# Hybrid decoder layer on one core: the output projection's weights placed and split beside the last branch map

## The chip, the core and the metric

The kernel runs on one core of a Trainium2 chip. The metric is the time of one execution on the device in microseconds (us), as the median of several runs; less is better. TensorE is called PE, VectorE DVE, ScalarE ACT, GpSimd POOL, and SyncE, which issues the loads, SP. The span is the stretch from the first to the last instruction of the profiled execution.

## What is computed

One layer on 256 tokens of width 4096, in float32. The parts that matter here:

```python
proj = rmsnorm(x, norm_g) @ w_in                    # 4096 -> 12288 columns, cut into eight sections
ya = conv_branch(a_val, a_glu, ...) @ a_pw          # width 1536: the big branch map, 1536 x 1536
ya = ya * silu(a_gate)
yb = gmlp_branch(b_u, b_v, ...) * silu(b_gate)      # width 1280
yc = pool_branch(c_in, c_w, ...) * silu(c_gate)     # width 1280
x = x + concat([ya, yb, yc]) @ w_out                # 4096 x 4096: the output projection
return rmsnorm(x, final_g)
```

## The kernel before

**Products in three passes.** Each float32 operand is split into two rounded parts: `hi`, a cast on ACT (L217 for weights, L291 for activations), and `lo`, the rest, a subtraction on DVE (L218, L292). A product is three matmuls of 128 x 128 by 128 x 512: hi·hi, hi·lo and lo·hi (L337 to L339; L864 to L866 in the paired columns). PE so reads weights only after ACT and then DVE have gone over them.

**Streaming.** Weights come in loads of 128 x 2048 floats, 1 MB (`Source.load`, L206). `stream` cuts a load into two sub-blocks of 1024 columns, splits each (`split`) and puts its use into a list `pending`, whose first entry is used when it holds more than AHEAD = 2. A sub-block is two input tiles of 128, for two groups of 128 tokens: 12 matmuls. In the front of the kernel the weights' pool `wpool` holds 4 raw loads and 3 split sub-blocks; in the back `wpool2` holds 3 raw loads and HELD = 5 split sub-blocks. The program is written in this order, and a scheduler then orders each engine's instructions by priority and by what they depend on. On the chip each engine goes through its own queue in order.

**Stages.** The input projection, the branches' element-wise work, the pooling branch's map, and then the big branch map `w_pw`: three groups of 512 columns, each six sub-blocks, from `project_rows` in a loop over `c0`. A group's result is multiplied into `a_gate` (L778), turned by transposes on PE (`turned`, L314) and split (L291, L292): these are `ya`, the last of the 32 input tiles of the output projection. Behind the loop stand `drain()`, which uses what is pending, `finish_all()`, and the closing of all pools of the front; only then are the back's pools opened: `xn` (the residual rows), `wpool2`, and the PSUM banks `q1` to `q8`.

**Output projection.** `first_columns` does columns 0 to 511: 16 sub-blocks, 192 matmuls, accumulated in banks `q2` and `q4`. In its course it makes eight `combine`s, sums of neighbouring activation blocks (L852, L856, L858, L859), and loads the residual rows (`load_rows`, L820 and L821). `rows_done` adds the result into `xn` on DVE (L829), squares it on ACT (L830), which frees the bank, and scales it (L835). `paired_columns` then does 1024 columns at a time, three times; in half of its steps seven products take the place of eight (a Strassen scheme), for which DVE also adds weight blocks (`w_sums`, L936 to L939). The last 512 columns are done in three pieces, with the final norm behind each token group: mean, square root on ACT (L975), reciprocal and scaling on DVE (L974 to L986), and the stores.

The square root's function table is loaded at the first use; `nc.scalar.activation(out=ssq[:, 0, 8:9], ..., func=AF.Sqrt)` (L813) is there for that alone.

Of the kernel before, what the change touches and what calls it, by code (L numbers as in the profile page):

```python
# [34 lines left out]
TAPS = 31  # L35
PAD = TAPS - 1
# [42 lines left out]
C_GROUP = W_C // len(POOL_WINDOWS)  # L79


OUT_BLOCKS = [0, 1, 2, 3, 4, 5, 6, 7]


PAIRED = [1, 3, 5, 6, 8, 10, 11, 13]


# [10 lines left out]
def trunk(ctx: ExitStack, tc: tile.TileContext, x, xt, params, w1, wv, w2, w_pw, w_c, w_o, wst, bbias, blg, blb, fg, out):  # L98
    nc = tc.nc

    const = ctx.enter_context(tc.tile_pool(name="const", bufs=1))
    acts = ctx.enter_context(tc.tile_pool(name="acts", bufs=1))
    front_ctx = ExitStack()
    weights = {"pool": front_ctx.enter_context(tc.tile_pool(name="wpool", bufs=1)), "raw": 4, "parts": 3}
    ps_acc = front_ctx.enter_context(tc.tile_pool(name="ps_acc", bufs=6, space=PSUM))
    ps_aux = front_ctx.enter_context(tc.tile_pool(name="ps_aux", bufs=2, space=PSUM))

    def raw_tile(name):
        return weights["pool"].tile([P, 2048], F32, tag="raw", name=name, bufs=weights["raw"])
# [49 lines left out]
    def finish_all():  # L159
        while urgent or slow:  # L160
            clock[0] += 1
            run_one()
# [25 lines left out]
    def drain():  # L188
        while pending:
            use_next()  # L190

    class Source:
# [6 lines left out]
        def load(self, n, parts=None):  # L199
            t = raw_tile("w_raw")  # L200
            at = 0
            if self.order:
                self.at = self.order.popleft() * P * 2048
            for w in parts or [n]:
                src = self.ap[self.at : self.at + P * w].rearrange("(p n) -> p n", p=P)
                nc.sync.dma_start(out=t[:, at : at + w], in_=src)  # L206
                last_load[:] = traced()[-1:]
                self.at += P * w
                at += w
            return t  # L210
# [152 lines left out]
    u_b = mid.tile([P, 2, W_B], F32, name="u_b")  # L363
    v = mid.tile([P, 2, W_B], F32, tag="m2", name="v")
    ws_sb = mid.tile([P, W_B], F32, tag="m3", name="ws_sb")
    h_a = mid.tile([P, TA, PAD + S], F32, tag="m1", name="h_a")
    late, tasks = {}, {}

    nc.gpsimd.memset(h_a[:, :, :PAD], 0.0)
# [102 lines left out]

    def post_a_gate(pss, col, o, w):
        if "a_gate" not in late:
            late["a_gate"] = mid.tile([P, 2, W_A], F32, tag="m1", name="a_gate")
        for c in range(2):
            yield from silu(late["a_gate"][:, c, col : col + w], pss[c][:, o : o + w], c)

# [303 lines left out]
        return evacuate  # L782

    src_pw = Source(w_pw)
    for c0 in range(0, W_A, 512):
        project_rows(src_pw, h_hl, 512, evacuate_pw(c0))
    drain()
    finish_all()
    mid_ctx.close()
    tmp_ctx.close()  # L790
    front_ctx.close()


    def back(**kw):
        return ctx.enter_context(tc.tile_pool(bufs=1, reuse_waits="tile", **kw))

    outp = back(name="outp")
    xn = outp.tile([P, 2, D], F32, name="xn")
    weights.update(pool=back(name="wpool2"), raw=3, parts=HELD)
    sums = weights["pool"]  # L800
    combos = [sums.tile([P, 4, 2, P], F32R, name=f"combo{i}") for i in range(len(PAIRED))]
    fin = back(name="fin")
    ssq = fin.tile([P, 2, 9], F32, name="ssq")
    ps_out = back(name="ps_out", space=PSUM)

    def bank(i):
        return ps_out.tile([P, 512], F32, tag=f"q{i}", name=f"q{i}", bufs=1)

    y_all = yb + yc + ya
    y_hl = [y_all[4 * b + i] for b in OUT_BLOCKS for i in range(4)]  # L810
    src_o = Source(w_o, [8 * g + b for g in (0, 7) for b in OUT_BLOCKS])

    nc.scalar.activation(out=ssq[:, 0, 8:9], in_=ones[:, :1], func=AF.Sqrt)  # L813
    LAST = D - 512
    fg_bc = {}

# [16 lines left out]
    def rows_done(c, ps, c0):  # L833
        z = add_rows(c, ps, c0, 512, c0 // 512)
        nc.vector.tensor_tensor(out=z, in0=z, in1=fg_bc[c0], op=ALU.mult)  # L835

    def scratch(name):

        return sums.tile([P, 4, 512], F32, tag="sums", name=name, bufs=1)

# [27 lines left out]
    def paired_columns(g):  # L868
# [51 lines left out]
        for p in range(KT // 2):  # L920
            if p == 4:
                load_rows(g * 512)
                load_rows((g + 1) * 512)
            raw = raw_tile("w_raw")
            for h in range(2):
                at = ((g + h) * 8 + OUT_BLOCKS[p // 2]) * P * 2048
                src = w_o[at : at + P * 2048].rearrange("(p n) -> p n", p=P)
                nc.sync.dma_start(out=raw[:, h * 1024 : (h + 1) * 1024], in_=src[:, (p % 2) * 1024 : (p % 2 + 1) * 1024])
            if p not in PAIRED:
                for h in range(2):  # L930
                    feed(*split(raw[:, h * 1024 : (h + 1) * 1024]), lambda a, b, p=p, h=h: plain(p, h, (a, b)))
                continue
            w = raw.rearrange("p (b n) -> p b n", b=4)
            s = scratch("w_sums")
            w57 = s[:, :2]
            nc.vector.tensor_tensor(out=w57, in0=w[:, 0::3], in1=w[:, 2:3].broadcast_to([P, 2, 512]), op=ALU.add)  # L936
            feed(*split(raw[:, :1024]), lambda a, b, p=p: seven(p, (1, 2), (a, b)))
            nc.vector.tensor_tensor(out=s[:, 2], in0=s[:, 0], in1=w[:, 3], op=ALU.add)
            nc.vector.tensor_tensor(out=s[:, 3], in0=s[:, 2], in1=w[:, 1], op=ALU.add)  # L939
            feed(*split(raw[:, 1536:]), lambda a, b, p=p: seven(p, (3,), (a, b)))  # L940
            flat = s.rearrange("p b n -> p (b n)")
            feed(*split(flat[:, :1024]), lambda a, b, p=p: seven(p, (5, 7), (a, b)))
            feed(*split(flat[:, 1024:]), lambda a, b, p=p: seven(p, (6, 4), (a, b)))

    def first_columns():

        acc = [bank(i) for i in (2, 4)]
        todo = deque(range(len(PAIRED)))

        def use(k0, nk, hi, lo):  # L950
            for c in range(2):
                for i in range(nk):
                    k = k0 + i
                    rows_product(acc[c], c, hi, lo, y_hl[k], i, 0, 512, k == 0, k == KT - 1)
            if todo and k0 % 4 == 2:
                combine(todo.popleft())
            if k0 == 8:
                load_rows(0)

        stream(src_o, KT, 512, use)  # L960
        drain()
        for c in range(2):
            rows_done(c, acc[c], 0)

    def mean_so_far(c, n):
        a = fin.tile([P, 1], F32, tag="fin_a", name="fin_a", bufs=2)
# [145 lines left out]
```

## Time and profile before

| | |
|---|---|
| median of 3 runs | 1380.23 us (1379.55 to 1381.44) |
| the profiled execution's own time | 1379.32 us |
| its span | 1377.6 us |
| mean granted clock of PE | 0.993 |
| busy, share of the span | PE 99%, PE weight loads 82%, DVE 75%, ACT 49% |
| moved by DMA | 281.01 MB, mean 204 GB/s |

A share of busy time is a mean over stages, so the views by stage and the timelines say more. In a timeline a row begins with its start (us from the start of the span) and its duration; `x2` says that two instructions were merged, and the bracket at the end how long the engine was idle before and what ended that. Matmuls overlap: one of 512 columns has a duration of 0.39 us, but at full clock the next one starts 0.23 us later, so times of PE are taken from start to start. `w_hi<-w_raw` is a cast of weights, `ps_acc` and `q` are accumulators.

### The profile page before, as it was taken

What the parts mean: (1) busy time and instruction counts of PE and PEld (TensorE: products, weight loads), DVE (VectorE), ACT (ScalarE), POOL (GpSimd) and SP (SyncE); (2) the same over time, 40 slices, a digit from 0 to 9 for tenths busy, and PEclk for the clock granted to TensorE, in tenths of its full rate; (3) what the DMA queues carried; (4) which work ended last, traced back from release to release, by engine and by line L of the source; (5) the groups of instructions that cost most, each with busy time, mean ns of one, the idle gap of its engine ahead of it and who ended that gap; (6) DMA issues with size and microseconds to landing.
All of it is one profiled execution on the core that took longest, in us unless ns stands there. A gap on an engine that the chain in (4) does not pass through costs nothing.

```text
span 1377.6 us, 16339 instructions
## 1 busy us (share of the span) xinstructions
PE 1357.2 (99%) x6224; PEld 1129.5 (82%) x6224; DVE 1034.3 (75%) x1468; ACT 677.5 (49%) x806; POOL 5.7 (0%) x52
## 2 busy tenths in 40 slices
PE   9999999999999999999999999999979999999996
PEld 7888888888988888888888888888868888888886
DVE  7568888888888887786447744567568899999974
ACT  8654444444445443564344443455444565656642
POOL 0000000000000000000000000000000000000000
PEclk9999999999999999999999999999989999999998
DMA  9975555555556555554555555555518755666663
GB/s 348 344 264 184 187 192 201 183 188 202 192 200 192 202 194 186 195 199 155 186 194 198 184 193 204 184 187 172 213 66 300 254 202 205 216 211 221 216 221 123
DMA packets 56591, 281.01 MB, mean 204 GB/s; under 512 B 8640, under 2 KB 12096, under 8 KB 31168
## 3 DMA queue, kind: packets, MB, share of 16 engines
q1 hardware_dynamic: 56368, 279.95, 57.8%
q8 instruction: 48, 0.79, 0.2%
q14 instruction: 31, 0.25, 0.1%
q10 hardware_dynamic: 144, 0.02, 0.0%
HBM read 275.75 MB, written 4.19 MB: 203 GB/s over the span
## 4 chain that ended last, share of the span: by engine, by line
PE 96%; DVE 2%; DMA 1%; ACT 0%; issue 0%; SPq 0%; DVEq 0%; ACTq 0%
PE ps_acc L338 24%; PE ps_acc L339 24%; PE ps_acc L337 24%; PE q L864 6%; PE q L865 6%; PE q L866 6%; PE q L338 2%; PE q L339 2%; PE q L337 2%; DMA gb<-in_blb_dram 1%; PE ps_aux L314 1%; DVE w_lo L218 0%; DVE xn L983 0%; DMA w_raw<-in_w_dram 0%; PE ps_aux L390 0%; PE ps_aux L612 0%
## 5 line engine op out<-in xcount | busy, mean ns | idle before, releaser
L218 DVE TENSOR_TENSOR w_lo<-w_raw,w_hi 128x1024 fp32r<-128x1024 f32 (+1 forms) x495 | 589.3, 1196 | 290.5 <-ACT w_hi L217 289.1
L217 ACT CAST w_hi<-w_raw 128x1024 fp32r<-128x1024 f32 (+1 forms) x495 | 506.3, 1030 | 563.2 <-PE ps_acc L339 315.1
L337 PE MATMUL ps_acc<-w_hi,act 128*128 128x512 f32 (+2 forms) x1504 | 578.4, 385 | 0.7 <-ACT w_hi L217 0.7
L338 PE MATMUL ps_acc<-w_lo,act 128*128 128x512 f32 (+2 forms) x1504 | 577.6, 384 | 0.4 <-DVE w_lo L218 0.3
L339 PE MATMUL ps_acc<-w_hi,act 128*128 128x512 f32 (+2 forms) x1504 | 577.8, 384 | 0.0
L338 PEld LDWEIGHTS ps_acc<-w_lo,act 128*128 128x128 f32 x1504 | 282.7, 188 | 56.4 <-DVE w_lo L218 1.7
L337 PEld LDWEIGHTS ps_acc<-w_hi,act 128*128 128x128 f32 x1504 | 282.5, 188 | 55.8 <-ACT w_hi L217 0.9
L339 PEld LDWEIGHTS ps_acc<-w_hi,act 128*128 128x128 f32 x1504 | 282.6, 188 | 55.1
L524 DVE SCALAR_TENSOR_TENSOR c_a<-h_a,par,c_a 128x256 f32<-128x256 f32 x360 | 153.7, 479 | 0.0
L864 PE MATMUL q<-w_hi,act 128*128 128x512 f32 x264 | 102.8, 390 | 0.0
L865 PE MATMUL q<-w_lo,act 128*128 128x512 f32 x264 | 102.7, 389 | 0.0
L866 PE MATMUL q<-w_hi,act 128*128 128x512 f32 x264 | 102.6, 389 | 0.0
L217 ACT CAST w_hi<-w_sums 128x1024 fp32r<-128x1024 f32 x48 | 50.6, 1054 | 55.7 <-DVE w_sums L939 28.1
L218 DVE TENSOR_TENSOR w_lo<-w_sums,w_hi 128x1024 fp32r<-128x1024 f32 x48 | 58.3, 1222 | 5.7 <-ACT w_hi L217 4.8
L337 PE MATMUL q<-w_hi,act 128*128 128x256 f32 (+1 forms) x160 | 56.3, 353 | 4.3 <-ACT w_hi L217 4.3
L864 PEld LDWEIGHTS q<-w_hi,act 128*128 128x128 f32 x264 | 49.5, 188 | 10.8 <-ACT q L830 0.6
L866 PEld LDWEIGHTS q<-w_hi,act 128*128 128x128 f32 x264 | 49.6, 188 | 10.4
L338 PE MATMUL q<-w_lo,act 128*128 128x256 f32 (+1 forms) x160 | 56.5, 353 | 1.5 <-DVE w_lo L218 1.5
L865 PEld LDWEIGHTS q<-w_lo,act 128*128 128x128 f32 x264 | 49.5, 188 | 10.1
L339 PE MATMUL q<-w_hi,act 128*128 128x256 f32 (+1 forms) x160 | 56.2, 351 | 0.0
L337 PEld LDWEIGHTS q<-w_hi,act 128*128 128x128 f32 x160 | 30.7, 193 | 8.5 <-ACT w_hi L217 4.5
L865 PE MATMUL q<-w_lo,combo 128*128 128x512 f32 x96 | 37.3, 389 | 0.0
(145 smaller groups left out, 664.5 us busy)
## 6 DMA issues: line engine op xcount, KB each, us to landing
w_raw<-in_w_dram SPq DMA_DIRECT2D x149, 1024.0 KB, 4.8
w_raw<-in_w_o_dram SPq DMA_DIRECT2D x96, 512.0 KB, 4.7
w_raw<-in_wv_dram SPq DMA_DIRECT2D x20, 1024.0 KB, 4.8
w_raw<-in_w_o_dram SPq DMA_DIRECT2D x16, 1024.0 KB, 5.6
w_raw<-in_w_pw_dram SPq DMA_DIRECT2D x9, 1024.0 KB, 4.8
x_rows<-in_x_dram SPq DMA_DIRECT2D x4, 1024.0 KB, 6.8
xn<-in_x_dram SPq DMA_DIRECT2D x8, 512.0 KB, 8.3
out_dram<-xn SPq DMA_DIRECT2D x6, 512.0 KB, 3.3
```

What stands on the lines that cost most here:

```text
L217: nc.scalar.copy(out=hi[:, w], in_=raw[:, w])
L218: nc.vector.tensor_tensor(out=lo[:, w], in0=raw[:, w], in1=f32(hi[:, w]), op=ALU.subtract)
L314: nc.tensor.transpose(ps[:, c * P : (c + 1) * P], rows[:, c, m * P : (m + 1) * P], ident)
L337: nc.tensor.matmul(ps[:, :w], lhsT=act[:, c, 0], rhs=hi, start=f, stop=False)
L338: nc.tensor.matmul(ps[:, :w], lhsT=act[:, c, 0], rhs=lo, start=False, stop=False)
L339: nc.tensor.matmul(ps[:, :w], lhsT=act[:, c, 1], rhs=hi, start=False, stop=l)
L524: nc.vector.scalar_tensor_tensor(out=c_a[:, m], in0=src, scalar=w, in1=c_a[:, m], op0=ALU.mult, op1=ALU.add)
L864: nc.tensor.matmul(ps, lhsT=ahi, rhs=hi, start=f, stop=False)
L865: nc.tensor.matmul(ps, lhsT=ahi, rhs=lo, start=False, stop=False)
L866: nc.tensor.matmul(ps, lhsT=alo, rhs=hi, start=False, stop=l)
```

## The change

All pools of SBUF's front that live until the last branch map (`wpool`, and a new pool `gate` for `h_a` and `a_gate`) are laid out from the right end. The middle pools lie at the left and are closed when the projection of group 1 has been written, before group 2's; `wpool2` is opened there at once, and the output projection's loads and splits follow the branch map in the stream, without `drain()` and `finish_all()`. `first_columns` accumulates in the front's PSUM pool. At its fourth sub-block (`k0 == 6`) it calls `branches_done`, which closes the front's pools and opens those of `xn`, the combinations and the final norm; the square root's first use stands there too. Combinations are made at `k0` = 10, 12, ..., 24 instead of 2, 6, ..., 30, and `load_rows(0)` at 12 instead of 8. Each load gets an ordering dependency, without a semaphore, on the one before. `OUT_BLOCKS`, the numbers 0 to 7 in order, is dropped. The diff without that and without renamings:

```diff
-    weights = {"pool": front_ctx.enter_context(tc.tile_pool(name="wpool", bufs=1)), "raw": 4, "parts": 3}
-    ps_acc = front_ctx.enter_context(tc.tile_pool(name="ps_acc", bufs=6, space=PSUM))
-    ps_aux = front_ctx.enter_context(tc.tile_pool(name="ps_aux", bufs=2, space=PSUM))
+    front_ctx, ps_ctx = ExitStack(), ExitStack()
+    weights = {"pool": front_ctx.enter_context(tc.tile_pool(name="wpool", bufs=1, side="right")), "raw": 4, "parts": 3}
+    gate = front_ctx.enter_context(tc.tile_pool(name="gate", bufs=1, side="right"))
+    ps_acc = ps_ctx.enter_context(tc.tile_pool(name="ps_acc", bufs=6, space=PSUM))
+    ps_aux = ps_ctx.enter_context(tc.tile_pool(name="ps_aux", bufs=2, space=PSUM))
...
+                if last_load:
+                    tc.add_manual_dep(traced()[-1], last_load[0].name, ISSUE_ORDER, reason="in the order of use")
                 last_load[:] = traced()[-1:]
...
     for c0 in range(0, W_A, 512):
         project_rows(src_pw, h_hl, 512, evacuate_pw(c0))
-    drain()
-    finish_all()
-    mid_ctx.close()
-    tmp_ctx.close()
-    front_ctx.close()
+        if c0 == 512:
+            finish_urgent()
+            mid_ctx.close()
+            tmp_ctx.close()
...
     weights.update(pool=back(name="wpool2"), raw=3, parts=HELD)
...
+    def branches_done():
+
+        nonlocal outp, fin, xn, ssq
+        finish_urgent()
+        assert not slow and len(ya) == TA
+        y_hl.extend(ya)
+        front_ctx.close()
+        outp = back(name="outp")
+        xn = outp.tile([P, 2, D], F32, name="xn")
+        combos.extend(outp.tile([P, 4, 2, P], F32R, name=f"combo{i}") for i in range(len(PAIRED)))
+        fin = back(name="fin")
+        ssq = fin.tile([P, 2, 9], F32, name="ssq")
+        nc.scalar.activation(out=ssq[:, 0, 8:9], in_=ones[:, :1], func=AF.Sqrt)
...
     def first_columns():

-        acc = [bank(i) for i in (2, 4)]
+        nonlocal ps_out
+        acc = [ps_acc.tile([P, 512], F32, name="ps_acc") for _ in range(2)]
         todo = deque(range(len(PAIRED)))

         def use(k0, nk, hi, lo):
+            if k0 == 6:
+                branches_done()
...
-            if todo and k0 % 4 == 2:
+            if todo and k0 >= 10:
                 combine(todo.popleft())
-            if k0 == 8:
+            if k0 == 12:
                 load_rows(0)
...
         for c in range(2):
             rows_done(c, acc[c], 0)
+        ps_ctx.close()
+        ps_out = back(name="ps_out", space=PSUM)
```

The lines of the changed kernel lie a little further down: L217 and L218 are L218 and L219 there, L291 is L292, L314 is L315, L337 to L339 are L338 to L340, L778 is L779, L813 is L819, L829 and L835 are L840 and L846, L936 to L939 are L947 to L950.

**ACT, from the branch map's last group to the output projection.** `w_hi` are casts of weights; those from `w_raw_7940` and `w_raw_7950` are the first of the output projection. Before:

```order
L217 CAST w_hi_7844<-w_raw_7826 128x1024
L291 CAST act_7781<-ps_aux_7778 128x2x128
L291 CAST act_7787<-ps_aux_7784 128x2x128
L291 CAST act_7889<-ps_aux_7886 128x2x128
L291 CAST act_7895<-ps_aux_7892 128x2x128
L291 CAST act_7901<-ps_aux_7898 128x2x128
L291 CAST act_7907<-ps_aux_7904 128x2x128
L858 CAST combo0_7922<-a_full_7984 128x4x128
L217 CAST w_hi_7942<-w_raw_7940 128x1024
L217 CAST w_hi_7946<-w_raw_7940 128x1024
L858 CAST combo1_7923<-a_full_8027 128x4x128
L217 CAST w_hi_7952<-w_raw_7950 128x1024
```

Now, in the middle of the last group (`w_raw_7870`, `w_raw_7930` and `w_raw_7964` are output weights, `w_raw_7735` and `w_raw_7795` branch map weights):

```order
L218 CAST w_hi_7737<-w_raw_7735 128x1024
L218 CAST w_hi_7872<-w_raw_7870 128x1024
L218 CAST w_hi_7753<-w_raw_7735 128x1024
L218 CAST w_hi_7888<-w_raw_7870 128x1024
L218 CAST w_hi_7932<-w_raw_7930 128x1024
L218 CAST w_hi_7797<-w_raw_7795 128x1024
L218 CAST w_hi_7948<-w_raw_7930 128x1024
```

The first output casts stood behind the last conversions and the first combination's cast; now they alternate with the casts of the branch map's last group; four of them stand in these rows and a fifth (`w_hi_7966`) a little further down the queue, all ahead of the last four conversions. DVE's subtractions moved in the same way. The load of the square root's table and its first use (L819) moved from the start of the program to the place just ahead of those four conversions.

**PE, from the last matmul of the branch map on.** `ps_aux` are transposes of the gated result, accumulators `q2` and `q4` (before) and `ps_acc_7868` and `ps_acc_7869` (now) belong to the output projection. Before:

```order
L339 MATMUL ps_acc_7803<-w_hi_7844,act_7081 128x512
L314 MATMUL ps_aux_7886<-ident_74,a_gate_6657 128x128
L314 MATMUL ps_aux_7892<-ident_74,a_gate_6657 128x128
L314 MATMUL ps_aux_7886<-ident_74,a_gate_6657 128x128
L314 MATMUL ps_aux_7892<-ident_74,a_gate_6657 128x128
L314 MATMUL ps_aux_7898<-ident_74,a_gate_6657 128x128 x2
L314 MATMUL ps_aux_7904<-ident_74,a_gate_6657 128x128 x2
L337 MATMUL q2_7938<-w_hi_7942,act_7219 128x512
L337 MATMUL q4_7939<-w_hi_7942,act_7219 128x512
```

Now:

```order
L340 MATMUL ps_acc_7808<-w_hi_7849,act_7084 128x512
L315 MATMUL ps_aux_7906<-ident_77,a_gate_6660 128x128
L315 MATMUL ps_aux_7912<-ident_77,a_gate_6660 128x128
L338 MATMUL ps_acc_7868<-w_hi_7872,act_7222 128x512
L339 MATMUL ps_acc_7868<-w_lo_7873,act_7222 128x512
L340 MATMUL ps_acc_7868<-w_hi_7872,act_7222 128x512
L315 MATMUL ps_aux_7906<-ident_77,a_gate_6660 128x128
L315 MATMUL ps_aux_7912<-ident_77,a_gate_6660 128x128
L338 MATMUL ps_acc_7868<-w_hi_7872,act_7228 128x512
L339 MATMUL ps_acc_7868<-w_lo_7873,act_7228 128x512
L340 MATMUL ps_acc_7868<-w_hi_7872,act_7228 128x512
L338 MATMUL ps_acc_7869<-w_hi_7872,act_7222 128x512
```

The eight transposes stood in one block ahead of the first output matmul; now output matmuls stand between them.

**DVE, at the end of `first_columns`.** `a_full` and `combo` are combinations, `w_sums` the paired columns' weight sums. Before:

```order
L856 TENSOR_TENSOR a_full<-a_full 128x128 x2
L218 TENSOR_TENSOR w_lo<-w_raw,w_hi 128x1024
L859 TENSOR_TENSOR combo_7929<-a_full,combo_7929 128x4x128
L936 TENSOR_TENSOR w_sums<-w_raw 128x1024
L218 TENSOR_TENSOR w_lo<-w_raw,w_hi 128x1024
L938 TENSOR_TENSOR w_sums<-w_sums,w_raw 128x512
L939 TENSOR_TENSOR w_sums<-w_sums,w_raw 128x512
L218 TENSOR_TENSOR w_lo<-w_raw,w_hi 128x1024
L218 TENSOR_TENSOR w_lo<-w_raw,w_hi 128x512
L829 TENSOR_TENSOR xn<-q_7938,xn 128x512
L829 TENSOR_TENSOR xn<-q_7939,xn 128x512
L835 TENSOR_TENSOR xn<-xn,fg_bc 128x512
```

Now:

```order
L867 TENSOR_TENSOR a_full<-a_full 128x128 x2
L219 TENSOR_TENSOR w_lo<-w_raw,w_hi 128x512
L867 TENSOR_TENSOR a_full<-a_full 128x128
L840 TENSOR_TENSOR xn<-ps_acc,xn 128x512
L867 TENSOR_TENSOR a_full<-a_full 128x128
L840 TENSOR_TENSOR xn<-ps_acc,xn 128x512
L846 TENSOR_TENSOR xn<-xn,fg_bc 128x512
L870 TENSOR_TENSOR combo_7999<-a_full,combo_7999 128x4x128
L846 TENSOR_TENSOR xn<-xn,fg_bc 128x512
L947 TENSOR_TENSOR w_sums<-w_raw 128x1024
```

The weight sums of the first pair stood ahead of the two additions into `xn`; now they stand behind them and behind the eighth combination.

## Rows read from the trace of the kernel before

**Rows 1.** chain of waits that ended last, share of the span by engine (the page)

```profile
PE 96%; DVE 2%; DMA 1%; ACT 0%; issue 0%; SPq 0%; DVEq 0%; ACTq 0%
```

**Rows 2.** busy time by stage: us; PE, PEld, DVE, ACT, POOL (instructions); PEclk; DMA; GB/s

```profile
1000.00:1021.60 21.60, 21.60 (x103) 17.23 (x102) 12.15 (x17) 7.93 (x13) 0.00 (x0) 1.00 0.19 80
1021.60:1031.50 9.90, 2.69 (x11) 1.13 (x9) 7.48 (x20) 5.01 (x9) 0.00 (x0) 0.65 0.00 0
...
1036.00:1076.40 40.40, 40.40 (x180) 33.27 (x178) 34.66 (x61) 18.91 (x23) 0.00 (x0) 1.00 0.87 312
1076.40:1166.00 89.60, 89.60 (x395) 73.94 (x395) 83.41 (x93) 52.73 (x63) 0.00 (x0) 1.00 0.61 208
1166.00:1248.00 82.00, 82.00 (x364) 67.89 (x363) 80.03 (x89) 49.20 (x58) 0.00 (x0) 1.00 0.63 213
```

**Rows 3.** the same view in steps of 2 us at the seam

```profile
1024.00:1026.00 2.00, 0.45 (x4) 0.20 (x2) 1.45 (x5) 0.71 (x2) 0.00 (x0) 0.63 0.00 0
1026.00:1028.00 2.00, 0.00 (x0) 0.00 (x0) 1.19 (x5) 0.88 (x2) 0.00 (x0) 0.50 0.00 0
...
1034.00:1036.00 2.00, 2.00 (x9) 1.59 (x8) 2.00 (x3) 0.40 (x1) 0.00 (x0) 0.81 0.76 307
```

**Rows 4.** PE timeline: start us, us, engine line op out<-in [idle before <-releaser]

```profile
1021.25 0.40 PE L339 MATMUL ps_acc<-w_hi,act 128*128 128x512 f32 x1
1021.48 0.38 PE L314 MATMUL ps_aux<-ident,a_gate 128*128 128x128 f32 x2
1022.42 0.44 PE L314 MATMUL ps_aux<-ident,a_gate 128*128 128x128 f32 x2 [0.56 <-DVE a_gate L778]
1023.67 0.77 PE L314 MATMUL ps_aux<-ident,a_gate 128*128 128x128 f32 x4 [0.81 <-DVE act L292]
1028.74 1.22 PE L337 MATMUL q<-w_hi,act 128*128 128x512 f32 x2 [4.29 <-ACT w_hi L217]
1031.50 0.80 PE L338 MATMUL q<-w_lo,act 128*128 128x512 f32 x1 [1.54 <-DVE w_lo L218]
...
1034.66 0.45 PE L337 MATMUL q<-w_hi,act 128*128 128x512 f32 x1
...
1076.22 0.84 PE L864 MATMUL q<-w_hi,act 128*128 128x512 f32 x2
...
1081.98 0.39 PE L864 MATMUL q<-w_hi,act 128*128 128x512 f32 x1
```

**Rows 5.** load queue's timeline, and time to landing of line L206's loads, 985 to 1036

```profile
992.99 39.95 SPq L206 DMA_DIRECT2D w_raw<-in_w_o_dram  x4
...
DMA to landing us min/median/max: 4.7/6.9/12.2
```

**Rows 6.** timelines of ACT and DVE at the seam

```profile
1022.79 0.65 ACT L291 CAST act<-ps_aux 128x256 fp32r<-128x256 f32 x2 [6.19 <-PE ps_aux L314]
...
1027.64 1.99 ACT L217 CAST w_hi<-w_raw 128x1024 fp32r<-128x1024 f32 x2
...
1030.23 2.35 DVE L218 TENSOR_TENSOR w_lo<-w_raw,w_hi 128x1024 fp32r<-128x1024 f32 x2
```

**Rows 7.** PE timeline inside the branch map's last group

```profile
1006.85 0.39 PE L314 MATMUL ps_aux<-ident,a_gate 128*128 128x128 f32 x2
...
1007.31 0.40 PE L337 MATMUL ps_acc<-w_hi,act 128*128 128x512 f32 x1
```

**Rows 8.** DVE timeline at the hand-over to the paired columns

```profile
1068.53 1.23 DVE L936 TENSOR_TENSOR w_sums<-w_raw 128x1024 f32<-128x1024 f32 x1
...
1076.42 0.69 DVE L829 TENSOR_TENSOR xn<-q,xn 128x512 f32<-128x512 f32 x1 [0.67 <-PE q L339]
```

**Rows 9.** timelines of ACT, PE and DVE on the tail

```profile
1360.83 1.28 ACT L975 ACT_TABLE_LOAD   x1
...
1366.23 0.28 PE L339 MATMUL q<-w_hi,act 128*128 128x256 f32 x1
...
1367.09 0.42 DVE L829 TENSOR_TENSOR xn<-q,xn 128x256 f32<-128x256 f32 x1
```

More of the change, by code (lines that the diff above doesn't have):

```diff
@@ L79 @@
 C_GROUP = W_C // len(POOL_WINDOWS)
-OUT_BLOCKS = [0, 1, 2, 3, 4, 5, 6, 7]
 PAIRED = [1, 3, 5, 6, 8, 10, 11, 13]
@@ L102, in trunk @@
     acts = ctx.enter_context(tc.tile_pool(name="acts", bufs=1))
-    front_ctx = ExitStack()
-    weights = {"pool": front_ctx.enter_context(tc.tile_pool(name="wpool", bufs=1)), "raw": 4, "parts": 3}
-    ps_acc = front_ctx.enter_context(tc.tile_pool(name="ps_acc", bufs=6, space=PSUM))
-    ps_aux = front_ctx.enter_context(tc.tile_pool(name="ps_aux", bufs=2, space=PSUM))
+    front_ctx, ps_ctx = ExitStack(), ExitStack()
[3 more added lines that the diff above has]
+    ps_aux = ps_ctx.enter_context(tc.tile_pool(name="ps_aux", bufs=2, space=PSUM))
     def raw_tile(name):
@@ L365, in trunk @@
     ws_sb = mid.tile([P, W_B], F32, tag="m3", name="ws_sb")
-    h_a = mid.tile([P, TA, PAD + S], F32, tag="m1", name="h_a")
+    h_a = gate.tile([P, TA, PAD + S], F32, tag="m1", name="h_a")
     late, tasks = {}, {}
@@ L474, in post_a_gate @@
         if "a_gate" not in late:
-            late["a_gate"] = mid.tile([P, 2, W_A], F32, tag="m1", name="a_gate")
+            late["a_gate"] = gate.tile([P, 2, W_A], F32, tag="m1", name="a_gate")
         for c in range(2):
@@ L784, in trunk, with finish_urgent @@
     src_pw = Source(w_pw)
+    def finish_urgent():
+        while urgent:
+            clock[0] += 1
+            run_one()
     for c0 in range(0, W_A, 512):
         project_rows(src_pw, h_hl, 512, evacuate_pw(c0))
-    drain()
-    finish_all()
-    mid_ctx.close()
-    tmp_ctx.close()
-    front_ctx.close()
+        if c0 == 512:
+            finish_urgent()
+            mid_ctx.close()
+            tmp_ctx.close()
     def back(**kw):
         return ctx.enter_context(tc.tile_pool(bufs=1, reuse_waits="tile", **kw))
-    outp = back(name="outp")
-    xn = outp.tile([P, 2, D], F32, name="xn")
     weights.update(pool=back(name="wpool2"), raw=3, parts=HELD)
[L800 to L804, printed above, removed]
+    outp = fin = xn = ssq = ps_out = None
+    y_hl, combos = yb + yc, []
+    def branches_done():
[10 more added lines that the diff above has]
+        nc.scalar.activation(out=ssq[:, 0, 8:9], in_=ones[:, :1], func=AF.Sqrt)
     def bank(i):
         return ps_out.tile([P, 512], F32, tag=f"q{i}", name=f"q{i}", bufs=1)
[L809 to L813, printed above, removed]
+    src_o = Source(w_o, [8 * g + b for g in (0, 7) for b in range(8)])
     LAST = D - 512
@@ L837, in scratch @@
     def scratch(name):
-        return sums.tile([P, 4, 512], F32, tag="sums", name=name, bufs=1)
+        return outp.tile([P, 4, 512], F32, tag="sums", name=name, bufs=1)
     def combine(i):
@@ L925, in paired_columns @@
             for h in range(2):
-                at = ((g + h) * 8 + OUT_BLOCKS[p // 2]) * P * 2048
+                at = ((g + h) * 8 + p // 2) * P * 2048
                 src = w_o[at : at + P * 2048].rearrange("(p n) -> p n", p=P)
```

## The prediction

> **What bounds the kernel now.** I read the chain of waits first, then the busy time by stage, then the timelines at the places where TensorE (PE) is not full. The chain is 96% PE [rows 1]: time is won only where PE waits or runs slowly, and work taken off another engine is worth nothing by itself. By stage, PE is busy for all 21.60 us before the end of the big branch map, for 2.69 of the next 9.90 us, and for the whole of every later stretch down to the last output columns [rows 2]. So there is one hole, the passage from the branch map to the output projection; call it the seam. In it the granted clock falls from 1.00 (2.4 GHz) to 0.50 (1.2 GHz), and it is 0.81 over 1034 to 1036 [rows 2, 3].
>
> The PE timeline shows what ends each wait [rows 4]. After the last branch matmul at 1021.25, eight transposes wait 0.56 and 0.81 us for the gate product and the conversions. Then PE waits 4.29 us for the first `w_hi` of the output weights and 1.54 us for its `w_lo`. The next matmuls start 0.43 us apart until the tenth at 1034.66. From there to the first paired matmul at 1076.22 are 183 starts in 41.56 us, 0.227 each. The weights are not late from HBM: of the four in the row that starts at 992.99 three go out at once and the fourth waits for a buffer; loads of this stretch land in 4.7 to 12.2 us [rows 5], and nothing moves in 1021.6 to 1031.5 [rows 2]. What is late is the splitting. ACT makes its first output `w_hi` at 1027.64, behind conversions and a combination's cast, though it had idled 6.19 us before 1022.79; DVE's first two `w_lo` come at 1030.23 [rows 6].
>
> **The change, part by part.**
>
> *The seam.* Five splits now stand in ACT's and DVE's queues between those of the branch map's last group (the order above). They need SBUF that the left side has free once group 1's projection no longer needs the middle pools, and raw tiles that have landed by about 1006 [rows 5]. Their price is 5 x 1.0 us on ACT and 5 x 1.2 on DVE [rows 6], in a stretch of 21.6 us where DVE works 12.15 and ACT 7.93 [rows 2]: both fit beside PE. Five sub-blocks are 5 x 12 matmuls x 0.227 = 13.6 us of work for PE, while ACT and DVE finish the last conversions and the sixth split. The two waits inside the transposes go too: three matmuls (0.68) now stand where PE waited 0.56, and six (1.36) where it waited 0.81.
>
> What this gives back: from the first transpose at 1021.48 to the tenth output matmul at 1034.66 are 13.18 us. At full clock the content is nine matmuls, 9 x 0.227 = 2.04, and four transpose pairs. A pair set into the stream with one matmul takes 0.46 us [rows 7], so 0.23 by itself, 0.92 for four. The excess is 13.18 - 2.04 - 0.92 = **10.2 us**. Bounds: it cannot give more than 10.2; the least is worked out with the rivals.
>
> *The combinations and the hand-over to the paired columns.* The eight combinations move from every fourth input tile to tiles 10 to 24 in the program, and DVE's queue ends differently: the additions into `xn` now stand ahead of the weight sums of the first pair, and the eighth combination lies around them. DVE is busy 34.66 of 40.40 us in this stretch [rows 2]; with the seam gone it does the same work in less time, so I expect it late. Before, its second addition starts right when PE's second accumulator is done, at 1076.42, and from 1076.22 to the 25th paired matmul at 1081.98 are 5.76 us for 24 starts, 5.44 at 0.227: PE loses 0.3 us where the paired products want that bank [rows 4, 8]. Late by one split, 1.2 us, the loss would be 1.2 us, **0.9 more**. Below: nothing, if DVE keeps up. Above: the sums (one operation of 1024 columns and two of 512) and one split, 1.23 + 2 x 0.69 + 1.2 = 3.8 [rows 6, 8]. I take 0.9, as the order moves one group of sums, which PE doesn't need at once, behind the additions, and one combination before them.
>
> *The table load.* The kernel loads the square root's table before it first needs it. That moves from program start to ACT's idle time before 1022.79 [rows 6], and then no other table comes, so the load of 1.28 us at 1360.83 on the tail goes [rows 9]. DVE waits for the root behind it, then scales the finished columns and takes the last addition at 1367.09, though PE's last matmul starts at 1366.23 and takes 0.28. Without the load that addition is held by PE alone, to about 1366.5. Gain **0.5 us**, and no more, as PE's end caps it, though the load is 1.28.
>
> *Edits at nothing.* The extra table load that this makes in the input stage, 1.28 us on ACT, and the earlier one that is gone at the start lie where ACT is ahead or waits for loads; if the cover were gone each would be 1.3 at most. `load_rows(0)` sits behind five weight loads on SP instead of four; its rows are wanted some 40 us later. The dependency that holds loads in program order issues nothing. `OUT_BLOCKS` was the identity. The change adds no instruction otherwise.
>
> *Sum.* 10.2 - 0.9 + 0.5 = 9.8 us. The profiled execution took 1379.32, so 1369.5; the median of the three runs is 0.9 above it, so **1370.4 us**.
>
> *A rule against it.* PE is not quite dense at the new seam: transposes there still wait for a gate product, an ACT cast and a DVE subtraction in turn. In the old seam the clock was at 0.63 already in 1024 to 1026, right after short waits of 0.56 and 0.81 us and before the long one was over [rows 3, 4]. The Trainium skill (TensorE: Matmul & The Clock Gate, A second HAM failure mode) says that many short idles between groups of matmuls can make the clock swing between its two levels, without one long wait. By that rule the clock could still fall here; the trace shows neither for nor against, as the long wait followed at once. The third rival prices it by rows: 1374.1 where the sum has 1370.4.
>
> **The rivals.**
>
> 1. *DVE becomes the bound behind the seam.* For it: DVE is busy 83.41 of 89.60 and 80.03 of 82.00 us in the first paired stretches [rows 2], so what it brings along late is worked off slowly, and the splits of the paired sums have PE right behind them. Against: its idle time there, 6.2 us in the first, is more than the 3.8 that moves. It would give back 1.5 to 5 us beyond the sum: 1372 to 1375.4.
>
> 2. *Slower: the early splits block the branch map.* ACT works in order, and its cast of the second output load now stands ahead of the cast of the third sub-block of the branch map's last group. That sub-block's matmuls begin four sub-blocks before 1021.48, 4 x 2.72 us, at 1010.6; cast and subtraction take 2.3, so ACT may wait until 1008.3. The loads land from about 999 to 1006 [rows 5]. Each microsecond past 1008.3 costs one; to be slower than before a load would have to come 10 us later still, past 1018. For it: a landing of 12.2 us exists. Against: that was the third of three queued transfers, with nothing else moving. At 1021, the time would be 1383.
>
> 3. *The seam shrinks but stays.* If the chain through the transposes holds PE as it did, that costs 1023.67 - 1021.48 less two pairs at 0.23, 1.7 us. If the clock then falls as before, seven starts take 3.16 instead of 1.59 us (1031.50 to 1034.66), and two in front 0.4 more: 2.0. Together 3.7 us lost, 1374.1 [rows 4, 7].
>
> 4. *The change doesn't do what it says.* If the splits wait for memory that comes free only with the last branch matmul, nothing but the tail is won: 1379.7. Against: the queues have them between the casts of the last group, and ACT and DVE could not pass them.
>
> **How the numbers follow.** The forecast has 0.64, with 1368.5 (no stall at all at the hand-over, 1.2, and the lowest run 0.7 under its median) to 1371.9 (the highest 1.2 above, and 0.3 for the rest); the first rival 0.20, the third 0.09, the fourth and small variants of it 0.03, the second 0.04. The range leaves out the second, the fourth and the far end of the first: 1368.5 to 1374.6. A measurement of this kernel tells about 0.2% from no change, 2.8 us. Faster by more than that: 0.64 + 0.20 + 0.09 = 0.93; within it 0.03; slower 0.04.
>
> **What would show it.** After the last branch matmul the timeline should have transposes in pairs with output matmuls between, none over 0.3 us late, the granted clock at 1.00 over the whole seam, and output casts on ACT before the last conversions. First paired matmul: some 10.2 us earlier, at 1066. A PE wait of about 1.2 us for an ACT square should stand shortly behind it, and no table load on the tail, the last addition at PE's end. I am wrong if the first paired matmul is at 1066 and the end comes less than 7 us earlier (then look for PE waits for DVE in the paired columns), or if a wait for `w_hi` stands inside the branch map.

## The result and the profile after

| | before | after |
|---|---|---|
| median | 1380.4 us (1379.55 to 1381.44, 4 runs) | 1393.12 us (1392.14 to 1394.02, 4 runs) |
| ratio, with 95% interval | | 1.0092 [1.0074, 1.0109] |
| the profiled execution | 1379.32 us, span 1377.6 | 1392.27 us, span 1390.5 |
| mean granted clock of PE | 0.993 | 0.997 |

The change makes the kernel 12.7 us slower; 1370.4 was predicted, and 1374.6 was the upper end of the range. First, four lines of the page: busy times, the chain of waits that ended last, and two groups of matmuls.

```profile
PE 1378.2 (99%) x6224; PEld 1133.2 (81%) x6224; DVE 1036.0 (75%) x1468; ACT 675.7 (49%) x806; POOL 5.7 (0%) x52
...
PE 99%; DVE 1%; ACT 0%; issue 0%; POOL 0%; ACTq 0%; POOLq 0%
...
L338 PE MATMUL ps_acc<-w_hi,act 128*128 128x512 f32 (+2 forms) x1568 | 611.9, 391 | 0.0
...
L875 PE MATMUL q<-w_hi,act 128*128 128x512 f32 x264 | 102.9, 390 | 0.7 <-ACT ps_acc L841 0.7
```

The chain is PE for 99%, where it was 96% [rows 1], and L875 is the only one of the large groups of matmuls with any idle time ahead of it. So the hole is gone, and the time is longer. The busy time by stage says the same at the seam. The first stretch is that of before [rows 2] 22.9 us later, the last one that of before 12.7 us later; what before took from 1021.6 to 1036.0 is here 1044.5 to 1048.4. Columns as there.

```profile
1022.90:1044.50 21.60, 21.60 (x102) 17.49 (x101) 16.71 (x22) 13.47 (x20) 0.00 (x0) 1.00 0.45 167
1044.50:1048.40 3.90, 3.90 (x23) 3.05 (x22) 2.02 (x5) 1.46 (x5) 0.00 (x0) 1.00 0.28 67
1048.40:1089.10 40.70, 40.70 (x181) 33.74 (x180) 34.98 (x71) 18.94 (x22) 0.00 (x0) 1.00 0.80 276
1089.10:1178.70 89.60, 88.86 (x393) 73.23 (x392) 86.07 (x98) 53.13 (x64) 0.00 (x0) 1.00 0.59 203
```

PE is full through the seam and the granted clock stays at 1.00, where 9.90 us held 2.69 of work and the clock fell to 0.50 [rows 2, 3]. The early splits are there too: DVE works 16.71 of the 21.60 us ahead of the seam instead of 12.15, ACT 13.47 instead of 7.93. The PE timeline at the seam and at the hand-over to the paired columns:

```profile
1044.15 0.40 PE L340 MATMUL ps_acc<-w_hi,act 128*128 128x512 f32 x1
1044.39 0.38 PE L315 MATMUL ps_aux<-ident,a_gate 128*128 128x128 f32 x2
1044.52 0.48 PE L338 MATMUL ps_acc<-w_hi,act 128*128 128x512 f32 x1
...
1045.33 0.44 PE L315 MATMUL ps_aux<-ident,a_gate 128*128 128x128 f32 x2
1045.52 0.48 PE L338 MATMUL ps_acc<-w_hi,act 128*128 128x512 f32 x1
...
1088.95 0.39 PE L875 MATMUL q<-w_hi,act 128*128 128x512 f32 x1
...
1090.08 0.39 PE L877 MATMUL q<-w_hi,act 128*128 128x512 f32 x1
1091.20 0.51 PE L875 MATMUL q<-w_hi,act 128*128 128x512 f32 x1 [0.74 <-ACT ps_acc L841]
```

From the first transposes at 1044.39 to the first paired matmul at 1088.95 are 44.56 us; before they were 1076.22 - 1021.48 = 54.74 [rows 4]. The seam thus gave 10.18 us. But its first transposes start 1044.39 - 1021.48 = 22.9 us later than before. **All of the loss lies in front of the seam, where the change was thought to do nothing.**

No wait stands there. What differs is how many matmuls fit into a stretch. Two windows in the front, after and then before:

```profile
100.00:150.00 50.00, 50.00 (x218) 40.58 (x217) 43.07 (x73) 20.46 (x22) 0.00 (x0) 1.00 0.51 181
500.00:550.00 50.00, 50.00 (x217) 40.57 (x216) 41.89 (x71) 21.95 (x26) 0.00 (x0) 1.00 0.54 189
```

```profile
100.00:150.00 50.00, 50.00 (x222) 41.42 (x221) 43.52 (x75) 21.13 (x21) 0.00 (x0) 1.00 0.53 190
500.00:550.00 50.00, 50.00 (x222) 41.42 (x221) 40.43 (x66) 21.98 (x26) 0.00 (x0) 1.00 0.53 189
```

PE is 100% busy in all four and the granted clock is 1.00 in all four, yet 2% fewer matmuls start. In the PE timeline, where nothing waits, the same eleven steps; after, then before:

```profile
299.74 0.39 PE L338 MATMUL ps_acc<-w_hi,act 128*128 128x512 f32 x1
...
302.29 0.40 PE L340 MATMUL ps_acc<-w_hi,act 128*128 128x512 f32 x1
```

```profile
299.66 0.39 PE L337 MATMUL ps_acc<-w_hi,act 128*128 128x512 f32 x1
...
302.15 0.39 PE L339 MATMUL ps_acc<-w_hi,act 128*128 128x512 f32 x1
```

Eleven starts take 2.55 us after, 0.232 each, and 2.49 before, 0.226 each. Start by start, matmuls of 512 columns in after are 228 to 241 ns apart, in a pattern that repeats every seven (229 and 238 in turn up to some 97 us); in before they are 226 or 227 except just behind a break in the stream, and so they are in after from 1048 us on. The view of groups, kept apart by shape, tells how many there are up to 1048 us (L339 and L340 have as many):

```profile
L338 PE MATMUL ps_acc<-w_hi,act 128*128 128x512 f32 x1420 | 562.6, 397 | 0.0
```

Over some 4,250 of them 22.9 us is 5.4 ns each. Neither the busy share nor the clock shows it. The page has a trace of it that is easily passed over: the mean duration of L338's group, 391 ns, was 385 in before (both mix shapes; for 512 columns alone, in front of the seam, it is 397 in the row above and 391 in before).

What the change alters for the matmuls of the front is only where their operands lie. The weights' pool moved to the right end of SBUF, the on-chip memory that holds the tiles. The addresses are fixed when the program is built (bytes in a partition; "distance" is from the activations' tiles, the stationary operand `lhsT` of a matmul, to the weights', the moving operand `rhs`):

| | activations | front `w_hi`, `w_lo` | distance modulo 256 | back `w_hi` | distance modulo 256 |
|---|---|---|---|---|---|
| before | 19552 | 117856, 130144 | 0 | 179296 | 0 |
| after | 19552 | 204768, 217056 | 128 | 109664 | 0 |

All other tiles of these kinds follow in steps that are multiples of 256. So the slow stretch is the one whose weights lie at 128 modulo 256 from the activations. That was the theory for the experiments. Two rivals: the right end as such is slow for PE, or the front is slowed by something else that the change moved (the loads' ordering, the early splits, other traffic).

### The profile page after: what moved, and what is told of

Read it like the earlier page. It is cut to its first block, busy times and chain, and to the rows that moved or that the text cites. A ratio compares the mean times of both kernels' runs of the same rounds, so it can differ in the third digit from the quotient of the medians.

```text
span 1390.5 us, 16340 instructions
## 1 busy us (share of the span) xinstructions
PE 1378.2 (99%) x6224; PEld 1133.2 (81%) x6224; DVE 1036.0 (75%) x1468; ACT 675.7 (49%) x806; POOL 5.7 (0%) x52
## 4 chain that ended last, share of the span: by engine, by line
PE 99%; DVE 1%; ACT 0%; issue 0%; POOL 0%; ACTq 0%; POOLq 0%
PE ps_acc L338 25%; PE ps_acc L339 25%; PE ps_acc L340 25%; PE q L875 6%; PE q L876 6%; PE q L877 6%; PE q L339 1%; PE q L338 1%; PE q L340 1%; PE ps_aux L315 1%; PE ps_aux L391 0%; PE ps_aux L613 0%; PE ps_aux L276 0%; DVE xn L999 0%; ACT ps_acc L841 0%; DVE w_lo L219 0%
## 5 line engine op out<-in xcount | busy, mean ns | idle before, releaser
L219 DVE TENSOR_TENSOR w_lo<-w_raw,w_hi 128x1024 fp32r<-128x1024 f32 (+1 forms) x495 | 589.0, 1195 | 307.5 <-ACT w_hi L218 305.9
L218 ACT CAST w_hi<-w_raw 128x1024 fp32r<-128x1024 f32 (+1 forms) x495 | 505.0, 1027 | 581.9 <-PE ps_acc L340 506.5
L338 PE MATMUL ps_acc<-w_hi,act 128*128 128x512 f32 (+2 forms) x1568 | 611.9, 391 | 0.0
L339 PE MATMUL ps_acc<-w_lo,act 128*128 128x512 f32 (+2 forms) x1568 | 610.6, 389 | 0.0
L340 PE MATMUL ps_acc<-w_hi,act 128*128 128x512 f32 (+2 forms) x1568 | 610.4, 389 | 0.0
L339 PEld LDWEIGHTS ps_acc<-w_lo,act 128*128 128x128 f32 x1568 | 295.7, 189 | 64.5 <-DVE w_lo L219 0.8
L340 PEld LDWEIGHTS ps_acc<-w_hi,act 128*128 128x128 f32 x1568 | 295.6, 189 | 64.4
L338 PEld LDWEIGHTS ps_acc<-w_hi,act 128*128 128x128 f32 x1568 | 295.6, 189 | 64.2 <-ACT act L295 0.4
L875 PE MATMUL q<-w_hi,act 128*128 128x512 f32 x264 | 102.9, 390 | 0.7 <-ACT ps_acc L841 0.7
L218 ACT CAST w_hi<-w_sums 128x1024 fp32r<-128x1024 f32 x48 | 50.6, 1054 | 56.3 <-DVE w_sums L950 28.5
L219 DVE TENSOR_TENSOR w_lo<-w_sums,w_hi 128x1024 fp32r<-128x1024 f32 x48 | 58.1, 1220 | 2.6 <-ACT w_hi L218 1.7
L875 PEld LDWEIGHTS q<-w_hi,act 128*128 128x128 f32 x264 | 49.6, 188 | 11.5 <-ACT ps_acc L841 1.2
L877 PEld LDWEIGHTS q<-w_hi,act 128*128 128x128 f32 x264 | 49.6, 188 | 10.3
L876 PEld LDWEIGHTS q<-w_lo,act 128*128 128x128 f32 x264 | 49.6, 188 | 10.2
L877 PE MATMUL q<-w_hi,combo 128*128 128x512 f32 x96 | 37.4, 389 | 0.0
L875 PE MATMUL q<-w_hi,combo 128*128 128x512 f32 x96 | 37.0, 389 | 0.0
L339 PE MATMUL q<-w_lo,act 128*128 128x256 f32 (+1 forms) x96 | 30.7, 320 | 0.0
L338 PE MATMUL q<-w_hi,act 128*128 128x256 f32 (+1 forms) x96 | 30.7, 319 | 0.0
```

What stands on the lines that cost most here:

```text
L218: nc.scalar.copy(out=hi[:, w], in_=raw[:, w])
L219: nc.vector.tensor_tensor(out=lo[:, w], in0=raw[:, w], in1=f32(hi[:, w]), op=ALU.subtract)
L338: nc.tensor.matmul(ps[:, :w], lhsT=act[:, c, 0], rhs=hi, start=f, stop=False)
L339: nc.tensor.matmul(ps[:, :w], lhsT=act[:, c, 0], rhs=lo, start=False, stop=False)
L340: nc.tensor.matmul(ps[:, :w], lhsT=act[:, c, 1], rhs=hi, start=False, stop=l)
L875: nc.tensor.matmul(ps, lhsT=ahi, rhs=hi, start=f, stop=False)
```

## The experiments

### 1. The right end with other addresses

```diff
+    shift = front_ctx.enter_context(tc.tile_pool(name="shift", bufs=1, side="right"))
+    shift.tile([P, 896 // 4], F32, name="shift")
     weights = {"pool": front_ctx.enter_context(tc.tile_pool(name="wpool", bufs=1, side="right")), "raw": 4, "parts": 3}
```

> The changed kernel, with 896 unused bytes per partition at the right end, so that all tiles of the right pools lie 896 bytes lower; nothing else moves, the order of instructions is the same. In the changed kernel the split weights of the front begin at 2016 modulo 2048 and the stationary tiles at 1120; here, as in the kernel before, both are at 1120. Theory address (a matmul is slower where its two operands lie at certain offsets to each other): the front's matmuls go back from 0.232 to 0.227 us a start, the 22.9 us lost before the first paired matmul go, and the time is about 1370. Theory place (what counts is that the weights lie at the far end of the memory): no change, 1393. Theory traffic (the loads and splits of the output weights, or another order of instructions, slow PE): no change, 1393.

Measured: 1372.37 us (1371.36 to 1373.02, 4 runs) where before had 1381.36; ratio 0.9932 [0.9912, 0.9951]. 896 bytes that nothing uses take 21 us off the changed kernel, and the front's matmuls start 0.227 us apart again, 222 in 50 us:

```profile
500.00:550.00 50.00, 50.00 (x222) 41.43 (x221) 41.52 (x70) 22.38 (x27) 0.00 (x0) 1.00 0.56 197
```

The right end as such is not slow. But, against what was expected, this run did not change addresses alone: with the pad the scheduler put some instructions in another order. The table load is back on the tail, and the stall at the hand-over is larger, as ACT's and PE's timelines show:

```profile
1354.53 1.28 ACT L993 ACT_TABLE_LOAD   x1
```

```profile
1069.38 0.39 PE L879 MATMUL q<-w_hi,act 128*128 128x512 f32 x1
1071.46 0.50 PE L877 MATMUL q<-w_hi,act 128*128 128x512 f32 x1 [1.70 <-ACT ps_acc L843]
```

So it doesn't settle the size, and the fourth and fifth runs were made with pads that leave the order of every engine as it is in after.

### 2. The kernel before with its weights moved by 896 bytes

```diff
     weights = {"pool": front_ctx.enter_context(tc.tile_pool(name="wpool", bufs=1)), "raw": 4, "parts": 3}
+    weights["pool"].tile([P, 896 // 4], F32, name="shift")
```

> The kernel before, with 896 unused bytes at the start of the front's weights' pool, so that its raw and split weights (and the middle pools) lie 896 bytes higher; the back is untouched and the order is the same. Theory address: matmuls of the front start 0.232 us apart, and the time grows by about the 23 us that the change lost, to 1403; the paired columns stay at 0.227. Theory place: no change, 1380, as the weights stay on the left. Theory traffic: no change, 1380.

Measured: 1403.63 us (1402.34 to 1404.93, 2 runs), ratio 1.016 [1.0133, 1.0187]. Nothing of the change is in this kernel, the order of instructions on every engine is that of before, the weights stay on the left, and it loses 22.3 us. Its front is slow and its back is not (busy time by stage):

```profile
500.00:550.00 50.00, 50.00 (x217) 40.54 (x216) 41.89 (x71) 21.93 (x26) 0.00 (x0) 1.00 0.53 189
1100.00:1150.00 50.00, 50.00 (x222) 41.27 (x221) 45.12 (x48) 29.13 (x32) 0.00 (x0) 1.00 0.62 211
```

The rivals fall: neither the side nor the loads' order nor the early splits are needed for the loss; the addresses do it.

### 3. Forty distances, PE alone

Blocks of 48 matmuls of 512 columns in the kernel's pattern of operands, with no other engine at work; the activations stand at two places, the weights at twenty distances from them.

```diff
+    for b, (a, d) in enumerate(GRID):
...
+                    act = a + 2048 * (2 * (s % 2) + i) + 1024 * c
+                    hi = a + d + 16384 + 2048 * i + 4096 * (s % 3)
...
+                        nc.tensor.matmul(ps, lhsT=part(act + 512 * h, P), rhs=part(hi + w, 512), start=n == 0, stop=n == COUNT - 1)
```

> Leaves out the whole computation: x is copied to the output, and PE does 40 blocks of 48 matmuls of 512 columns on data already in SBUF, while no other engine works. Two places of the stationary tiles (1120 and 2016 modulo 2048) and for each 20 offsets of the moving operand to them, 0 to 2016 bytes. Theory address: 0.227 us a start at offset 0 and 0.232 at 896, in a pattern over the offsets that says whether the distance of the operands or the place of the moving one counts (if the distance, both places give the same pattern; if the place, the second is shifted by 896). Theory place and theory traffic: 0.227 in all blocks.

Three neighbouring blocks in the PE timeline, for distances 256, 384 and 512 (48 matmuls are merged into a row):

```profile
77.89 11.11 PE L126 MATMUL b<-field 128*128 128x512 f32 x48
...
88.90 11.37 PE L126 MATMUL b<-field 128*128 128x512 f32 x48
...
100.17 11.11 PE L126 MATMUL b<-field 128*128 128x512 f32 x48
```

The middle block takes 0.26 us more for 47 starts, 5.5 ns each. Mean time from start to start, worked out from the starts in the trace; the first 14 of each block, which are irregular behind the break between blocks, are left out:

| distance | activations at the kernel's place | activations 896 bytes on |
|---|---|---|
| 0, 256, 512, ... 1792 | 226.67 ns (227.33 for the first block of the run) | 226.67 ns |
| 128 | 233.18 | 233.21 |
| 384, 640, ... 1920 | 232.12 | 233.2 |
| 32 | 233.33 | 233.39 |
| 64 | 228.91 | 228.91 |
| 96 | 233.33 | 233.33 |
| 2016 | 233.30 | 233.27 |

The distance counts, modulo 256, and not the place. The odd multiples of 128 show the kernel's own two patterns, seven starts of 228 to 241 (mean 232.1), and 229 and 238 in turn (233.2); which of the two comes at a given distance stays open. At 232.12 the loss is 5.45 ns per matmul; times some 4,250 that is 23 us, and 22.9 were lost.

### 4 and 5. The changed kernel, with 128 and with 256 bytes of padding

```diff
+    shift = front_ctx.enter_context(tc.tile_pool(name="shift", bufs=1, side="right"))
+    shift.tile([P, 128 // 4], F32, name="shift")
```

> The changed kernel with 128 unused bytes per partition at the right end: the right pools lie 128 bytes lower and nothing else moves; every engine's queue holds the same instructions in the same order as in the changed kernel. The distance of the front's weights to the stationary tiles is then 768 modulo 2048, 0 modulo 256. Theory address, modulo 256: matmuls of the front start 0.227 us apart; against the kernel before: 10.2 us won at the seam, 0.5 on the tail, 0.6 lost at the hand-over (0.9 there in place of 0.3), so 10.1 faster, about 1370.5. Theory address, modulo a larger step (512 or more): still 0.232, 1393. Theory of the order of instructions: 1393.

> The control of the run with 128 bytes: 256 unused bytes at the right end, the same order again, distance 640 modulo 2048, 128 modulo 256. Theory address, modulo 256: 0.232 us a start in the front and 1393 as in the changed kernel. If the unused bytes help for another reason (a place that the DMA or DVE likes better): about 1370 here too.

Measured: with 128 bytes 1370.21 us (1369.29 to 1371.09, 5 runs), ratio 0.9923 [0.9911, 0.9936]; with 256 bytes (the same edit with 256 for 128) 1393.13 us (1392.78 to 1393.49, 2 runs), ratio 1.009 [1.0072, 1.0109]. Instructions and their order on every engine are those of after in both; the larger pad leaves the distance at 128 modulo 256, the smaller one makes it 0. Busy time by stage, first with 128, then with 256 bytes:

```profile
500.00:550.00 50.00, 50.00 (x222) 41.39 (x221) 40.53 (x66) 21.98 (x26) 0.00 (x0) 1.00 0.54 189
```

```profile
500.00:550.00 50.00, 50.00 (x216) 40.23 (x215) 41.53 (x69) 21.56 (x27) 0.00 (x0) 1.00 0.53 187
```

The 128-byte kernel is the change without the accident of its addresses, so its trace shows what the change itself is worth. PE's and DVE's timelines, at the seam, the hand-over and the tail:

```profile
1021.51 0.38 PE L317 MATMUL ps_aux<-ident,a_gate 128*128 128x128 f32 x2
...
1066.07 0.39 PE L877 MATMUL q<-w_hi,act 128*128 128x512 f32 x1
...
1067.21 0.39 PE L879 MATMUL q<-w_hi,act 128*128 128x512 f32 x1
1068.34 0.50 PE L877 MATMUL q<-w_hi,act 128*128 128x512 f32 x1 [0.74 <-ACT ps_acc L843]
...
1356.81 0.28 PE L342 MATMUL q<-w_hi,act 128*128 128x256 f32 x1
```

```profile
1357.12 0.42 DVE L842 TENSOR_TENSOR xn<-q,xn 128x256 f32<-128x256 f32 x1 [0.36 <-PE q L342]
```

### 6. Other banks for the first columns

The changed kernel takes the accumulators of the first columns from the front's pool in PSUM, the memory of the accumulators, and the paired columns want the first of these banks by their seventh matmul. Three small matmuls at the start of the 128-byte kernel, whose results nobody reads, move the first columns' accumulators to two other banks, which the paired columns reach later.

```diff
+    for _ in range(3):
+        nc.tensor.matmul(ps_acc.tile([P, 512], F32, name="ps_acc")[:, :P], lhsT=ones, rhs=ones, start=True, stop=True)
```

> The run with 128 bytes, and three matmuls more on constants at the start, while PE waits for the first loads: by them the rotation of the accumulators moves on by three, and those of the first 512 columns lie in the banks that the paired columns want at their 25th matmul and later instead of at the 7th. Theory hand-over (the additions and squares that DVE and ACT do late hold PE by the bank): the wait of PE for the square, 0.9 us in the changed kernel, goes, and the time is 0.5 to 0.9 below that of the run with 128 bytes. Rival (DVE is late with the split of the first weight sums as well, right behind): the wait moves to that split, and the time is the same within 0.3.

Measured: 1368.93 us (1368.07 to 1370.18, 5 runs), ratio to before 0.9914 [0.9901, 0.9928]. ACT's two squares come as late as they did, but PE no longer waits for them: the seventh paired matmul starts at 1068.48, in step with the others. ACT's timeline of the 128-byte kernel, then of this one, and this one's PE:

```profile
1066.43 0.60 ACT L843 ACTIVATE ps_acc<-xn 128x512 f32<-128x512 f32 x1 [2.21 <-DVE xn L842]
...
1067.06 0.60 ACT L871 CAST combo<-a_full 128x512 fp32r<-128x512 f32 x1
1067.57 0.59 ACT L843 ACTIVATE ps_acc<-xn 128x512 f32<-128x512 f32 x1
```

```profile
1068.62 0.59 ACT L845 ACTIVATE ps_acc<-xn 128x512 f32<-128x512 f32 x1
```

```profile
1067.12 0.39 PE L879 MATMUL q<-w_hi,act 128*128 128x512 f32 x1
...
1068.26 0.39 PE L881 MATMUL q<-w_hi,act 128*128 128x512 f32 x1
1068.48 0.39 PE L879 MATMUL q<-w_hi,act 128*128 128x512 f32 x1
1068.71 0.39 PE L880 MATMUL q<-w_lo,act 128*128 128x512 f32 x1
```

From the first to the 25th paired matmul are 5.44 us here, 6.48 in the 128-byte kernel and 5.76 in before: the stall of 1.04 us is gone. In the profiled executions that gain is hidden by a first paired matmul that starts 1.05 us later, and 0.84 of that is there at 9 us already: the three added matmuls move PE's first product from 5.20 to 5.84, and an early cast of weights on ACT, which waits for its load, starts at 8.02 instead of 7.15. Whether the edit or chance made the loads late was not separated. The medians of five runs each are 1.3 us apart, where 0.5 to 0.9 was expected, but the runs overlap (1368.07 to 1370.18 against 1369.29 to 1371.09): the gain at the hand-over is shown, the size of the gain in time is not. This version has the lowest median of all, ahead of both kernels.

### 7. Finer distances, and which matmuls suffer

> Leaves out the whole computation, like the first run of this kind: blocks of 96 matmuls on data in SBUF and nothing beside. The moving operand's distance to the stationary one in steps of 4 to 32 bytes up to 252; two blocks where only the third of the matmuls that reads the second weight tile is off, by 64 and by 128; two blocks where the stationary tiles change every 16 matmuls between distance 0 and 128; 256 columns at distance 0 and 128. If each matmul is slowed by its own pair of addresses: with a third of them off by 128 a mean of about 0.2285 us a start (a third of the 5.5 to 6.5 ns that all lose), and in the blocks of runs 16 starts at 0.227 and 16 slow ones in turn. If what counts is whether any one is off, since one slow start disturbs the next: more than a third. Within 32 bytes either no change (a coarse step) or a slow start at once (an exact match is wanted); I expect no change below 32.

The third run's blocks with 96 matmuls each, in finer steps of the distance, and blocks in which only some of the matmuls are off:

```diff
+            if kind == "all" or kind == "lo" and m == 1:
+                w += d
+            if kind == "runs" and n // 16 % 2:
+                act += d
```

Four blocks in the PE timeline: all matmuls at distance 64, all at 128, then only those that read `lo` weights at 64, and at 128 (the others at 0):

```profile
133.24 22.20 PE L128 MATMUL b<-field 128*128 128x512 f32 x96
...
177.85 22.61 PE L128 MATMUL b<-field 128*128 128x512 f32 x96
...
312.93 22.49 PE L128 MATMUL b<-field 128*128 128x512 f32 x96
...
335.32 22.40 PE L128 MATMUL b<-field 128*128 128x512 f32 x96
```

Mean ns from start to start, the first 16 starts of each block left out:

| distance | 0 | 4 | 8 | 16 | 32 | 64 | 96 | 128 | 160 | 192 | 224 | 240 | 252 |
|---|---|---|---|---|---|---|---|---|---|---|---|---|---|
| ns | 226.8 | 237.4 | 232.9 | 231.6 | 233.3 | 228.9 | 233.4 | 233.3 | 234.2 | 233.4 | 233.4 | 236.7 | 229.6 |

I had expected the small distances to be as good as 0: wrong. Of the distances tried, only an exact match modulo 256 runs at 226.7, and 4 bytes off it is the slowest of all. With only the `lo` third of the weights off by 128, the mean is 231.06; each slow matmul paying for itself would have given about 228.9 (a third of the way from 226.7 to 233.3). With that third off by 64 it is 231.9, slower than the 228.9 of the block in which all are off by 64. So a matmul's own distance doesn't give its time alone: a change of distance from one matmul to the next costs as well. In runs of 16 matmuls that alternate between distances 0 and 128, the first ten or so of a good run are still irregular. Matmuls of 256 columns take 120.0 ns at distance 0 and at 128, the two tried with them.

## Why the prediction was wrong

The term that failed is none of the sum's: it is the sentence "The change adds no instruction otherwise" under **Edits at nothing**, which puts the rest of the change at nothing without a reason. The move of the front's weights to the right end was named in the description of the change and then given no price and no bound. By the addresses that it makes it costs 22.9 us (1393.12, and 1370.21 with 128 bytes of padding), more than twice all that the change gives. The range missed for the same reason: its bounds covered the terms that were listed. Neither of the two signs of being wrong that the prediction named came: the first paired matmul was not at 1066 but at 1088.95, and no wait for a `w_hi` stands inside the branch map.

The listed terms, each headed by what the prediction gave it, by the trace of the 128-byte kernel, which has the change and the old distance:

- **Seam, 10.2 gained.** First transposes to first paired matmul: 1066.07 - 1021.51 = 44.56 us, where before took 54.74 [rows 4], 10.18 less. In after itself the same stretch takes the same 44.56. Output matmuls stand between the transposes, the longest wait of a transpose is some hundredths of a microsecond, and the clock stays at 1.00.
- **Hand-over, 0.9 lost.** The predicted stall of 1.2 us was 1.04, held by ACT's square as named. The first 25 paired matmuls take 6.48 us instead of 5.76: 0.7 lost. The sixth run shows what decides it: the bank, not DVE's lateness alone.
- **Tail, 0.5 gained.** No table load stands there; the one that was moved is at 1039.40 in after, ahead of the last conversions. The last addition starts 0.31 us behind the start of PE's last matmul, where it was 0.86 [rows 9]: 0.55 gained, capped by PE as said.
- **The other edits at nothing.** In front of the seam nothing is lost once the distance is back: the first transposes start at 1021.51, where they started at 1021.48 [rows 4]. The moved table loads and the order of the loads cost nothing that shows.
- **Sum, 9.8 gained.** 10.15 earlier at the first paired matmul, less 0.72, and 0.55, are 10.0 us; the span went from 1377.6 to 1367.6. The median, 1370.21, is 0.2 from the forecast of 1370.4, and that closeness is in part luck: the runs of before beside it had a median of 1380.81, 0.6 above the one that the forecast started from. In after the same steps give 12.73 later at the first paired matmul, 0.75 more at the hand-over and 0.54 back on the tail, 12.9 us, and its span is 12.9 us longer.

The rivals: DVE as the bound behind the seam did not come; it works 86.07 of 89.60 us in the first paired stretch and PE waits there once, at the hand-over. The early splits did not block the branch map, in which PE is full. The third, a seam that shrinks but keeps its waits and loses the clock, did not come either: PE is full over the seam at a granted clock of 1.00. The rule of the Trainium skill beside that rival (TensorE: Matmul & The Clock Gate, A second HAM failure mode) speaks of many short idles; the new seam has none, so no run here tries it. The rival that ended on the slower side had the wrong mechanism; the slower result came from a thing that was on no list.

Could the profile of before have told? Not the size: all matmuls that read weights lie at distance 0 modulo 256 in before, and no row of it shows another. What it could tell is that 4,250 matmuls in front of the seam have no slack at all, so that anything which touches each of them, operands' addresses included, needs a bound of its own: 1% of 227 ns on each is 9.6 us, as much as the whole gain.

## What to carry to other kernels

An edit that issues nothing can still move every operand: when a change lays out memory anew, compare the addresses of what the dense loop reads, and count starts in a dense window of both kernels (218 against 222 in 50 us here), because the busy share and the granted clock look the same at either pace. Where matmuls of 512 columns stand back to back, as here, place all moving operands at a multiple of 256 bytes from the stationary ones; a pad of 128 bytes was worth 23 us. And when one experiment's pad also reorders the program, look for another pad that doesn't before reading a size from it.

## What the hardware showed that was not expected

- Back-to-back float32 matmuls of 128 x 512 (the rounded kind of this kernel) start 226.67 ns apart when the addresses of stationary and moving operand agree modulo 256, and 228.9 to 237.4 ns apart at every other distance tried; at 256 columns, 120.0 ns at both distances tried. It is there with PE alone at work, so it needs no other engine and no transfer beside it. Why the distance counts was not separated by a run, and stays open.
- The slow pace has fixed patterns (seven starts of 228 to 241 ns, or 229 and 238 in turn), and when the distance changes from 128 back to 0 the even pace of 226 to 227 comes back only after some ten matmuls, 224 to 240 ns apart until then.
